# The last part's tail loads its weight chunks unsplit and splits them on the chip

## The chip, the cores and the metric

One core of a Trainium2 chip runs the whole kernel. The metric is the device time of one execution in microseconds (us); lower is better. Engine names follow the profile: PE is TensorE, DVE is VectorE, ACT is ScalarE, POOL is GpSimd, SP is SyncE, which here only issues transfers (DMAs).

## The reference

One step of a decoder layer for 1024 prompt tokens and 32 sample tokens with 1024 features, all in float32:

```
h = rms_norm(x);  z = h @ w_in                     # attention (8 heads) and a gated recurrence (4 heads)
x += concat([rms_norm(A), gated B]) @ w_out        # w_out 1024 x 1024
x += cross_attention(rms_norm(x), mem) @ w_co      # w_cq 1024 x 512, w_co 512 x 1024
h3 = rms_norm(x);  q = h3 @ w_pq                   # w_pq 1024 x 2048: 8 heads x 2 x 128
s1, s2 = q[..., :128] . k1, q[..., 128:] . k2      # top 16 of each, then top 16 of their sums
x += sum over 8 heads x 16 experts of  softmax(score) * gelu(h3 . peer_u[e]) * peer_v[e]
y = rms_norm(x)
```

## The kernel before

Products in float32 are made of three faster products: `split` (L168) writes a rounded copy `hi` (ACT, L169) and the rest `lo = src - hi` (DVE, L170), and `mm3` adds hi.hi, hi.lo and lo.hi (L201 to L203). The 1024 prompt tokens are handled in three parts of three, two and three blocks of 128 (the 32 sample tokens belong to the second). Each part has a middle (attention and recurrence) and a tail: w_out, w_cq, cross-attention, w_co, the norm h3, and then 16 chunks of w_pq, each followed by a product with the keys and `top16` on DVE (L917 to L921). In each tail a weight chunk is `project`ed at a time.

`load_w` (L179) loads such a chunk in halves of 128 x 512. The first part loads the weights themselves, splits them and stores both pieces in device memory (`wd`); the later parts load both stored pieces, in one DMA per half (L186), into the tile `wz` (three buffers in the last part). PE reads `wz` and nothing else touches it.

Beside the last part's tail run the last two `gates`: they turn the chosen experts of a block into a table, with two DVE instructions per four tokens (L1024, L1027), a PE product (L1032) and a copy (L1034), and store it (`gtall`). Five blocks of 128 tokens use all experts in the `dense` loop that follows: 128 steps, each with two halves: PE makes `a` (L201 to L203), ACT the gelu (L1088), DVE multiplies by the gate (L1090) and splits (L169, L170), PE adds into `y` and `yr` (L1098 to L1100). At its end the sums are normed and stored (L1138 to L1153). The other blocks (the sample tokens, then blocks 7, 6 and 5) fetch their experts a row of 128 x 1024 at a time: POOL issues an indirect DMA (L1183), DVE uses the row (L1190 for `peer_u`, L1201 for `peer_v`). These gathers run beside the end of the last tail and beside the dense loop; each block's own needs its experts chosen first (`select_tile`, which ends with L986). The sample's result is finished last (`finish_sample`, L1208).

The program is laid out ahead of time by a scheduler, which sets the order of each engine's queue from its own estimate; on the chip each engine works through its queue in that order. One `DVE` queue therefore serves the gates, the top 16, the gathers, the dense loop and the final norms.

## Time and profile before

| | us |
|---|---|
| median of 3 runs (lowest, highest) | 3629.08 (3626.5, 3631.28) |
| profiled execution, own time | 3627.68 |
| its span in the profile | 3625.8 |
| last part's tail: first and last stored-weight load of it issued | 1137.0 to 1726.0 |
| first and last gate multiply (L1090) of the dense loop | 1757.5 to 3562.5 |

The span is what the instructions cover; the own time is 1.9 us more. Times in the rows are counted from the span's start.

### The profile page before, as it was taken

How to read it: one execution, taken by the hardware profiler on the slowest of the kernel's cores; microseconds unless marked ns; L12 is line 12 of the kernel's file. 1: busy time of each engine (PE TensorE's matmuls, PEld its weight loads, DVE VectorE, ACT ScalarE, POOL GpSimd, SP SyncE). 2: the span in 40 equal slices, each digit the busy share in tenths (PEclk: the TensorE clock that was granted, in tenths of full speed). 3: DMA queues.
4: the chain of work that ended last, by engine and by line, in shares of the span. 5: the costliest groups of instructions: out<-in, count | busy, mean ns of one | idle time of the engine just before them, and what ended most of it. 6: DMA issues, size and time to landing. Idle time of an engine off the chain costs nothing.

```text
span 3625.8 us, 52725 instructions
## 1 busy us (share of the span) xinstructions
PE 3373.7 (93%) x19343; PEld 2912.4 (80%) x19343; DVE 2634.7 (73%) x5868; ACT 1220.6 (34%) x2282; POOL 1112.5 (31%) x871
## 2 busy tenths in 40 slices
PE   5999999999999889887799999999999999999994
PEld 4886776677887788777788998999888898988893
DVE  4443333243885687897888878988888898888997
ACT  4544344344434443431242222222222222222221
POOL 0000000000000000021316644656566565565555
PEclk9999999999999999898999999999999999999997
DMA  7667777656655485499659988999999999999998
GB/s 243 230 226 248 239 247 240 202 181 220 210 192 201 179 293 209 150 338 344 229 169 348 341 291 286 364 351 337 340 335 351 345 333 342 337 343 332 329 328 296
DMA packets 408514, 1007.82 MB, mean 278 GB/s; under 512 B 43968, under 2 KB 168896, under 8 KB 406848
## 3 DMA queue, kind: packets, MB, share of 16 engines
q1 hardware_dynamic: 288448, 568.20, 45.6%
q0 software_dynamic: 119808, 436.26, 33.0%
q8 instruction: 152, 2.49, 0.3%
q14 instruction: 106, 0.87, 0.1%
HBM read 866.01 MB, written 138.31 MB: 277 GB/s over the span
## 4 chain that ended last, share of the span: by engine, by line
PE 71%; DVE 10%; DMA 9%; issue 4%; ACT 3%; POOL 1%; SPq 1%; POOLq 0%; DVEq 0%; ACTq 0%
PE a L201 7%; PE a L203 7%; PE a L202 7%; PE y L1098 4%; PE y L1099 4%; PE y L1100 4%; PE z L201 4%; PE z L202 3%; PE z L203 3%; PE yr L1098 3%; PE yr L1099 2%; PE yr L1100 2%; PE y L201 2%; PE y L202 2%; PE y L203 2%
## 5 line engine op out<-in xcount | busy, mean ns | idle before, releaser
L1183 POOL DMA_INDIRECT row<-in_peer_u,ix x416 | 534.6, 1285 | 635.9 <-DVE dots L1190 347.6
L1183 POOL DMA_INDIRECT row<-in_peer_v,ix x416 | 543.1, 1306 | 412.1 <-DVE ha L1201 266.5
L201 PE MATMUL a<-xh,u 128*128 128x320 f32 x2048 | 636.8, 311 | 21.2 <-ACT w L1088 18.0
L203 PE MATMUL a<-xh,u 128*128 128x320 f32 x2048 | 634.5, 310 | 0.7 <-DVE u L170 0.7
L202 PE MATMUL a<-xl,u 128*128 128x320 f32 x2048 | 634.1, 310 | 0.0
L1201 DVE SCALAR_TENSOR_TENSOR ha<-row,dots,ha 128x1024 f32<-128x1024 f32 x416 | 533.0, 1281 | 22.2 <-DMA row<-in_peer_v,ix 17.8
L1190 DVE CUSTOM_DVE_ANT_0 row<-row,ha 128x1024 f32<-128x1024 f32 x416 | 497.9, 1221 | 39.5 <-DMA row<-in_peer_u,ix 39.5
L210 POOL TENSOR_TENSOR rs_r<-rs_m,mhalf 128x3 f32<-128x3 f32 (+2 forms) x25 | 23.4, 944 | 1369.7 <-DVE rs_m L208 1250.2
L1088 ACT ACTIVATE w<-a 128x320 f32<-128x320 f32 x256 | 111.6, 436 | 937.3 <-PE a L203 917.1
L201 PEld LDWEIGHTS a<-xh,u 128*128 128x128 f32 x2048 | 385.6, 188 | 40.5 <-ACT w L1088 25.8
L202 PEld LDWEIGHTS a<-xl,u 128*128 128x128 f32 x2048 | 385.7, 188 | 8.8
L203 PEld LDWEIGHTS a<-xh,u 128*128 128x128 f32 x2048 | 385.5, 188 | 2.8 <-DVE u L170 1.0
L201 PE MATMUL z<-zhi,wz 128*128 128x384 f32 (+2 forms) x928 | 330.4, 356 | 43.0 <-DMA wz<-wd_w_pq 16.2
L202 PE MATMUL z<-zlo,wz 128*128 128x384 f32 (+2 forms) x928 | 316.8, 341 | 3.4 <-DVE zlo L170 1.9
L203 PE MATMUL z<-zhi,wz 128*128 128x384 f32 (+2 forms) x928 | 314.0, 338 | 0.0
L1099 PE MATMUL y<-v,w 128*128 128x512 f32 x768 | 294.6, 392 | 0.0
L1098 PE MATMUL y<-v,w 128*128 128x512 f32 x768 | 269.6, 393 | 12.6 <-ACT v L169 11.2
L1100 PE MATMUL y<-v,w 128*128 128x512 f32 x768 | 264.5, 391 | 1.3 <-DVE w L170 1.2
L201 PEld LDWEIGHTS z<-zhi,wz 128*128 128x128 f32 x928 | 181.0, 195 | 87.3 <-issue 21.7
L1098 PE MATMUL yr<-v,w 128*128 128x512 f32 x512 | 201.8, 394 | 13.5 <-DVE ys L1127 11.7
L169 ACT CAST w<-w 128x320 fp32r<-128x320 f32 x256 | 117.8, 460 | 259.0 <-DVE w L1090 258.5
L1100 PE MATMUL yr<-v,w 128*128 128x512 f32 x512 | 199.9, 390 | 0.7 <-DVE w L170 0.7
(470 smaller groups left out, 6685.2 us busy)
## 6 DMA issues: line engine op xcount, KB each, us to landing
u<-in_uT SPq DMA_DIRECT2D x128, 512.0 KB, 7.0
v<-in_peer_v SPq DMA_DIRECT2D x128, 512.0 KB, 7.6
wz<-wd_w_in SPq DMA_DIRECT2D x112, 512.0 KB, 4.3
gt<-gtall SPq DMA_DIRECT2D x124, 320.0 KB, 10.8
wd_w_in<-wz SPq DMA_DIRECT2D x56, 512.0 KB, 3.2
gtall<-sg SPq DMA_DIRECT2D x34, 512.0 KB, 4.1
wd_w_pq<-wt SPq DMA_DIRECT2D x32, 512.0 KB, 3.1
wt<-wd_w_pq SPq DMA_DIRECT2D x32, 512.0 KB, 4.5
```

The source lines that it names most:

```text
L169: S.copy(hi, src)
L201: PE.matmul(out, lhsT=whi, rhs=xhi[:, c, sl], start=c == 0, stop=False)
L202: PE.matmul(out, lhsT=whi, rhs=xlo[:, c, sl], start=False, stop=False)
L203: ins = PE.matmul(out, lhsT=wlo, rhs=xhi[:, c, sl], start=False, stop=c == kc - 1)
L210: G.tensor_tensor(r, m, mhalf[:, :n], op=ALU.pow)
L1088: S.activation(ga[:, lo:hi], pa, AF.Gelu)
L1098: PE.matmul(o, lhsT=wh[:, sl], rhs=vh[:, ds], start=start and q == 0, stop=False)
L1099: PE.matmul(o, lhsT=wh[:, sl], rhs=vl[:, ds], start=False, stop=False)
L1100: PE.matmul(o, lhsT=wl[:, sl], rhs=vh[:, ds], start=False, stop=stop and q == len(ws) - 1)
L1183: G.indirect_dma_start(out=row, out_offset=None, in_=tab, in_offset=bass.IndirectOffsetOnAxis(ap=col(ix, j), axis=0))
L1190: V.tensor_tensor_reduce(row, row, hn, 1.0, 0.0, op0=ALU.mult, op1=ALU.add, accum_out=col(dots, j))
L1201: V.scalar_tensor_tensor(acc, row, col(dots, j), acc, op0=ALU.mult, op1=ALU.add)
```

## The change

Only the last part's tail changes (`pi == 2`). Its weights come by a new function `load_raw`: the weights themselves, a whole chunk in one DMA, into a buffer that attention no longer needs (`vn` for odd chunks, `kT` for even ones, one buffer each), and then one `split` per half into `wz`.

```
+    def load_raw(name, c, kc, tag):
+        raw = T(wk, [128, 8, 128], F32, "vn", 1) if c % 2 else T(wk, [128, 1024], F32, "kT").rearrange("p (c n) -> p c n", n=128)
+        SP.dma_start(raw[:, :kc], A[name][c])
+        out = []
+        for i in range(kc // 4):
+            w = T(wk, [128, 2, 4, 128], F32R, tag, 3)
+            split(w[:, 0], w[:, 1], raw[:, 4 * i : 4 * i + 4])
             out.append((w[:, 0], w[:, 1]))
         return out
...
             put = lambda name, kc, x, evac: [
-                project(load_w(name, c, kc, g["w"]), x, kc, N, lambda p: evac(c, p), g["bank"] + "y")
+                project((load_raw if pi == 2 else load_w)(name, c, kc, g["w"]), x, kc, N, lambda p: evac(c, p), g["bank"] + "y")
                 for c in range(A[name].shape[0])]
...
-                project(load_w("w_pq", jc, 8, g["w"]), h3, 8, N, lambda p: ANY.tensor_copy(q[:, :N], p),
+                project((load_raw if pi == 2 else load_w)("w_pq", jc, 8, g["w"]), h3, 8, N, lambda p: ANY.tensor_copy(q[:, :N], p),
                         g["bank"] + "y")
```

With it the scheduler lays out the queues anew from the last tail on. In the changed kernel lines from L194 on have numbers 10 higher.

SP's queue in the middle of the last tail's w_pq chunks, before (`wd_w_pq` are the stored pieces, `xh`, `xl`, `u`, `gt` are the dense loop's first loads, `gtall` the gates' stores):

```order
L186 DMA wz_15166<-wd_w_pq_0_1462_6805 128x1024
L1036 DMA gtall_165<-thi_14723 128x2048
L186 DMA wz_15168<-wd_w_pq_1_1465_6812 128x1024
L186 DMA wz_15218<-wd_w_pq_0_1472_6867 128x1024
L1047 DMA xh_15700<-h3x_65_163 128x1280
L1047 DMA xl_15701<-h3x_66_164 128x1280
```

And the changed kernel at the same chunks:

```order
L199 DMA kT_15262<-in_w_pq 128x1024
L1046 DMA gtall_165<-sg_14353 128x1024
L1046 DMA gtall_165<-sg_14354 128x1024
L199 DMA vn_15318<-in_w_pq 128x1024
L199 DMA kT_15376<-in_w_pq 128x1024
L1046 DMA gtall_165<-thi_14455 128x2048
```

One load now brings a whole chunk where two did, and a load into `kT` or `vn` must wait until DVE has split what lay there.

DVE's queue just ahead of the dense loop's first gate multiply, before (`vals` and `f` are the top 16 of the last w_pq chunk, `tw`, `sc`, `ci` belong to the selection of block 5, `ha<-row` is a gather row of the sample):

```order
L921 MAX_INDEX vals_14850<-vals_14850,f_15670 128x8 x2
L949 CAST ixb_15961<-vals_14850 128x256
L917 MAX sc_15907<-tw_15909 128x8 x8
L1201 SCALAR_TENSOR_TENSOR ha_29739<-row_29768,dots_29642,ha_29739 128x1024
L918 MAX_INDEX ci_15908<-sc_15907,tw_15909 128x8 x2
L1090 TENSOR_TENSOR w_15744<-w_15744,gt_15725 128x320
```

And in the changed kernel (its gate multiply is L1100, its gather row L1211):

```order
L970 TENSOR_TENSOR tw_16107<-tw_16107,ixb_16097 128x2048
L972 TENSOR_TENSOR tw_16100<-tw_16100 128x128x4
L971 TENSOR_TENSOR tw_16107<-tw_16107 128x128x8
L959 CAST ixb_16270<-vals_14922 128x256
L973 TENSOR_REDUCE c_3339_16099<-tw_16100 128x128
L170 TENSOR_TENSOR v_15877<-v_15874,v_15876 128x1024
L1100 TENSOR_TENSOR w_15880<-w_15880,gt_15861 128x320
```

Nearly all of block 5's selection now stands ahead of the first gate multiply, where before it had only begun.

DVE's queue from the dense loop's last split of a gated half (`w`) on, before (`ha<-row` are gather rows, `ys` and `u` sums of the dense blocks, L1152 the scaling by a norm):

```order
L170 TENSOR_TENSOR w_29431<-w_29429,w_29430 128x320
L1201 SCALAR_TENSOR_TENSOR ha_31808<-row_32133,dots_31423,ha_31808 128x1024
L1127 TENSOR_TENSOR ys_3268_15716<-ys_3268_15716,yr_29517 128x512
L1148 TENSOR_SCALAR fst_29580<-fst_29580 128x1
L1201 SCALAR_TENSOR_TENSOR ha_31808<-row_32136,dots_31423,ha_31808 128x1024
L1201 SCALAR_TENSOR_TENSOR ha_31808<-row_32139,dots_31423,ha_31808 128x1024
L1201 SCALAR_TENSOR_TENSOR ha_31808<-row_32142,dots_31423,ha_31808 128x1024
L1127 TENSOR_TENSOR ys_3268_15716<-ys_3268_15716,yr_29534 128x512
```

And in the changed kernel:

```order
L170 TENSOR_TENSOR w_29567<-w_29565,w_29566 128x320
L1148 TENSOR_TENSOR u_29712<-u_29712,y_3299_15847 128x512
L1137 TENSOR_TENSOR ys_3304_15852<-ys_3304_15852,yr_29653 128x512
L1158 TENSOR_SCALAR fst_29716<-fst_29716 128x1
L1162 SCALAR_TENSOR_TENSOR u_29712<-u_29712,fst_29716,u_29721 128x1024
L1148 TENSOR_TENSOR u_29725<-u_29725,y_3300_15848 128x512
```

Before, gather rows of the last block stand between the final sums and norms; in the changed kernel none is left by then.

## Rows read from the trace of the kernel before

**Rows 1.** The page: busy time by engine, and its shares in 40 slices of the span.

```profile
PE 3373.7 (93%) x19343; PEld 2912.4 (80%) x19343; DVE 2634.7 (73%) x5868; ACT 1220.6 (34%) x2282; POOL 1112.5 (31%) x871
...
DVE  4443333243885687897888878988888898888997
...
DMA  7667777656655485499659988999999999999998
```

**Rows 2.** Busy time in stretches from the last tail to the dense loop.

```profile
core 0: us, PE busy (x) PEld busy (x) DVE busy (x) ACT busy (x) POOL busy (x), PEclk, DMA share, GB/s
...
1300.00:1417.00 117.00, 112.22 (x778) 106.13 (x778) 87.22 (x358) 37.07 (x103) 0.00 (x0) 0.94 0.76 261
1417.00:1569.00 152.00, 125.62 (x799) 116.70 (x797) 132.26 (x421) 66.69 (x148) 9.58 (x9) 0.90 0.52 185
1569.00:1668.00 99.00, 83.09 (x532) 78.37 (x532) 97.90 (x305) 33.91 (x72) 20.92 (x18) 0.93 0.96 359
1668.00:1758.00 90.00, 56.08 (x284) 51.06 (x283) 60.09 (x267) 12.65 (x23) 16.92 (x18) 0.82 0.85 297
...
1900.00:3560.00 1660.00, 1633.50 (x9126) 1477.58 (x9125) 1431.40 (x1956) 430.29 (x707) 973.98 (x753) 1.00 0.93 335
```

**Rows 3.** The stored weights by tile: the last tail's loads, and who waited.

```profile
L186 SPq DMA_DIRECT2D wz<-wd_w_out x16: 319/320/1130, 1137.0 to 1430.1; - x16
...
L186 SPq DMA_DIRECT2D wz<-wd_w_cq x8: 319/319/320, 1433.7 to 1468.6; - x8
...
L186 SPq DMA_DIRECT2D wz<-wd_w_co x8: 319/320/722, 1472.4 to 1554.8; - x8
...
L186 SPq DMA_DIRECT2D wz<-wd_w_pq x32: 319/320/3084, 1559.4 to 1726.0; - x32
...
  PE z L201: 16.2, 6
```

**Rows 4.** Groups by line up to 1137 us: the same split, in the first part (busy, mean ns).

```profile
L170 DVE TENSOR_TENSOR wz<-raw,wz 128x512 fp32r<-128x512 f32 x56 | 38.7, 691 | 73.3 <-ACT wz L169 69.1 <-DMA wd_w_in<-wz 2.8 <-DMA raw<-in_w_in 1.2
...
L169 ACT CAST wz<-raw 128x512 fp32r<-128x512 f32 x56 | 34.6, 618 | 52.0 <-PE z L203 27.7 <-DMA raw<-in_w_in 11.6 <-DVE hq L452 6.8
```

**Rows 5.** DVE in order of time, in the last tail: two 128x512 instructions in succession.

```profile
1631.01 0.69 DVE L1024 TENSOR_TENSOR raw<-iota,x_vs 128x512 f32<-128x512 f32 x1
1631.61 0.69 DVE L1027 TENSOR_TENSOR oh<-high,low 128x512 f32<-128x512 f32 x1
```

**Rows 6.** DVE in order of time: adding the fifth chunk of w_out, in the last tail.

```profile
1417.33 0.56 DVE L551 TENSOR_TENSOR res<-z,res 128x384 f32<-128x384 f32 x1 [1.30 <-PE z L203]
```

**Rows 7.** Groups by line from 1430 us: a gather row, and two kinds of selection work.

```profile
L1201 DVE SCALAR_TENSOR_TENSOR ha<-row,dots,ha 128x1024 f32<-128x1024 f32 x416 | 533.0, 1281 | 22.2 <-DMA row<-in_peer_v,ix 17.8
...
L960 DVE TENSOR_TENSOR tw<-tw,ixb 128x2048 bf16<-128x2048 bf16 x10 | 12.2, 1222 | 0.0
...
L919 DVE MATCH_REPLACE8 tw<-sc,tw 128x100 f32<-128x100 f32 x42 | 10.0, 246 | 0.0
```

**Rows 8.** The gate multiplies by line: count, durations, first and last start.

```profile
L1090 DVE TENSOR_TENSOR w<-w,gt x256: 468/491/549, 1757.5 to 3562.5; 128x320 f32<-128x320 f32 x128
```

**Rows 9.** DVE, SP's queue and PE in order of time, from the last split on.

```profile
3565.34 0.54 DVE L170 TENSOR_TENSOR w<-w,w 128x320 fp32r<-128x320 f32 x1
...
3574.60 1.28 DVE L1152 SCALAR_TENSOR_TENSOR u<-u,fst,u 128x1024 f32<-128x1024 f32 x1
...
3588.90 1.28 DVE L1152 SCALAR_TENSOR_TENSOR u<-u,fst,u 128x1024 f32<-128x1024 f32 x1
...
3602.17 1.28 DVE L1201 SCALAR_TENSOR_TENSOR ha<-row,dots,ha 128x1024 f32<-128x1024 f32 x1 [1.46 <-DMA row<-in_peer_v,ix]
...
3604.75 1.28 DVE L1152 SCALAR_TENSOR_TENSOR u<-u,fst,u 128x1024 f32<-128x1024 f32 x1
...
3606.98 0.72 SPq L1210 DMA_DIRECT2D u<-accd  x1
...
3613.74 1.89 PE L1214 MATMUL yr<-u,sum 128*32 128x512 f32 x2 [34.88 <-DMA u<-accd]
```

More of the change, by code (lines that the diff above doesn't have):

```diff
@@ L193, in load_w @@
                     SP.dma_start(wd[name, c, i], w.bitcast(F32))
+            out.append((w[:, 0], w[:, 1]))
+        return out
+    def load_raw(name, c, kc, tag):
[5 more added lines that the diff above has]
+            split(w[:, 0], w[:, 1], raw[:, 4 * i : 4 * i + 4])
             out.append((w[:, 0], w[:, 1]))
```

## The prediction

> **What bounds the kernel now.** I read the page first. Over the whole span PE is busy 93% and DVE 73%, but both are averages: from about the middle on DVE and the transfers stand at eight or nine tenths in nearly every slice [rows 1]. So I cut the span into stretches around the changed tail [rows 2]. Up to 1417 us PE sets the pace (112 of 117 us), and DVE has 30 us idle. From 1417 to 1569 DVE is busy 132.3 of 152 us, idle 19.7. From 1569 to 1668 it is busy 97.9 of 99: DVE is full there, with the gates, the top 16 and the gathers in one queue, while the transfers too are at 0.96. From 1668 until the first gate multiply at 1757.5, DVE idles 29.9 of 90 us; here PE waits 16.2 us in six waits for stored w_pq pieces [rows 3], and the other engines wait behind it. So the last tail is bound by DVE's queue up to 1668 and by the weight loads after it. From the first gate multiply on PE rules: it is busy 1633.5 of 1660 us [rows 2], and the 256 gate multiplies come 1805/255 = 7.08 us apart [rows 8]. Whatever delays the first of them delays them all. At the end it is DVE's queue again, in which 21 gather rows stand behind the last split (counted in the order), and final norms between them [rows 9].
>
> **What is removed.** The last tail issues 16 + 8 + 8 + 32 = 64 loads of 512 KB, 33.6 MB [rows 3]. They become 36 (8, 4, 8 and 16; those of w_co hold 256 KB), 16.8 MB. At the 359 GB/s of 1569 to 1668 that is 47 us of transfer time less, but only its w_pq half falls where transfers are short.
>
> **What is added.** 64 splits of 128 x 512. On ACT a cast takes 0.62 us, 40 us in all [rows 4]; ACT is busy 33.9 of 99 us in the full stretch [rows 2], so that is hidden, unless a cast waits for its load at the head of ACT's queue. On DVE the subtraction takes 0.69 us [rows 4], and two such instructions in succession start 0.60 apart [rows 5]: 64 x 0.60 = 38.4 us.
>
> **What moves.** I counted DVE's new order up to the first gate multiply. Beside the splits it holds six more gather rows, at 1.2 each (1.28 less the overlap of 0.08) 7.2 us [rows 7]; most of block 5's selection, 30 top-16 instructions at about 0.25 and index work of which four take 1.14 [rows 7], in all about 16; and six evacuation copies that ACT made before, about 3. With the splits: 65 us more DVE work ahead of the first gate multiply. The six rows and the selection are work that DVE no longer has to do later, but later PE sets the pace, so doing it early gives nothing back there.
>
> **Delay of the dense loop.** About 4 of the 65 us stand ahead of the fifth w_out chunk at 1417.33 [rows 6], where PE is the slower one and DVE has room: nothing. The other 61 fall into 1417 to 1758, with 50.7 us of DVE idle to take them. Which idle can be used? The 29.9 us after 1668 come from late weights; with half the bytes, and w_pq chunks split several chunks ahead of their top 16 in the new order, I let 25 of them go. The 19.7 us before 1569 are waits for ACT's exponentials in cross-attention and for the first gather row; some splits now stand in between, so I take half, 10. Against that stand new waits of a subtraction for its cast: 56 such splits in the first part waited 69.1 us for ACT, 1.2 each, where DVE had nothing else to do [rows 4]. The bounds are 0 and 79 us; in a queue that is full the cast is usually done by the time DVE gets there, so I take the low end, 4. Delay: 61 - 25 - 10 + 4 = 30 us. Its bounds: all idle used, 61 - 50.7 = 10; only 25 used and 15 of cast waits, about 50.
>
> **The end.** From the end of the dense loop's last split (3565.9) to the span's end at 3625.8 there are 59.9 us. Each of the three norms of the kept blocks ends behind gather rows (scalings at 3574.60, 3588.90 and 3604.75), and the sample's finish can only load its sum after the third (3606.98) and runs to the end [rows 9]. In the new order no gather row is left there: 21 x 1.2 = 25.2 us of DVE work is gone from the chain. The norms still follow each other through ACT, POOL and a store each, so I take 36 us for what remains (bounds 34.7, if all 25.2 come off, and 45): 24 us less. This is the return of the gathers having gone ahead by those rows relative to the dense loop.
>
> **The dense loop itself** then holds about 20 gather rows more. DVE has 229 us idle in 1660 there and the transfers are at 0.93 [rows 2], 20 rows are 24 us of DVE and 10.5 MB. Hidden would be 0; all on the path 24. I take 4.
>
> **Sum.** +30 - 24 + 4 = +10 us. The profiled execution's own time is 3627.7, so 3637.7; the median of the runs stands 1.4 above it, so the median after is about 3639, 0.3% slower.
>
> **Rivals.**
> *The loads were the bound (faster).* PE waits for weights are the only waits in this tail that the change aims at. If the 61 us of DVE work could all slip into idle time (with casts and gathers never late), the delay would be 10 us or less, the sum -10 to -20: 3609 to 3619. The point that decides is a delay of 13 us: below it the time falls by over 0.2%. For it speak the 16.2 us of PE waits and DMA at 0.96; against it the stretch with DVE at 97.9 of 99, which has 1.1 us to give.
> The Trainium skill, Perfetto Trace Analysis, "Identifying the Most-Contended Engine", says to look for the engine with the highest occupancy and improve that one. Read over the whole span that is PE and the added DVE work costs nothing, which would make this rival the forecast, at about 3609; its "Optimization Strategy" adds that the most contended engine can change between regimes, and the rows by stretch show DVE at 99% in one of them, so I side with the stretch.
> *It cancels.* A delay of 13 to 27 us against the 24 at the end: within 0.2% (7 us), which is about what a measurement of this kernel can tell from no change. About 3629.
> *The raw buffers hold the queues (much slower).* `kT` and `vn` have one buffer each. A load waits for DVE's split of two chunks before; SP stands still meanwhile, and the gates' stores and the dense loop's first loads are queued behind it; ACT's cast at the head of its queue holds back the copies that empty PE's banks. With 15 us of waits for casts and no idle recovered before 1569, the delay is 50: 3660. For it speaks that DVE is the late engine, so each buffer comes free late; against it, that the loads stand four to six chunks ahead of the top 16 they serve.
>
> **Chances.** The forecast (delay 27 to 40, 3636 to 3650) 0.46; cancelled 0.26; faster 0.14; much slower 0.14. Slower by over 0.2%: 0.60; within: 0.26; faster: 0.14. Range for 8 in 10: from the middle of the faster rival to the slower one's own time, 3614 to 3660.
>
> **What would show it.** DVE near full from about 1417 until the first gate multiply, that multiply at about 1787 (1770 to 1800) instead of 1757.5, and PE's wait for w_pq weights gone or turned into a wait for the split. The gate multiplies 7.1 us apart as before, the last one about 30 later. The last gather row ahead of the last split, and some 36 us from there to the end. I would be wrong if DVE still had 30 us idle near the end of the tail, if the first multiply came before 1770, if the multiplies drew apart (the gathers then press on the loop), or if the end still took 50 us or more.

## The result and the profile after

The change makes the kernel slower: 3662.22 us (median of 7 runs, 3648.0 to 3672.07) against 3631.28 (7 runs, 3626.5 to 3639.34), a ratio of 1.0081 with a 95% interval of 1.0061 to 1.01. The profiled execution took 3665.35 us, with a span of 3663.6, which is 37.8 more than before; by the medians it is 30.9 more. Lines behind line 193 stand ten lower than in the kernel before (L1090 is L1100 now, L1024 is L1034).

The page, as [rows 1]:

```profile
PE 3401.0 (93%) x19343; PEld 2930.7 (80%) x19343; DVE 2675.8 (73%) x5939; ACT 1256.2 (34%) x2339; POOL 1114.3 (30%) x871
```

Busy time in stretches, as [rows 2], with one more for what is now ahead of the first gate multiply:

```profile
1417.00:1569.00 152.00, 126.71 (x795) 117.25 (x794) 143.15 (x460) 78.66 (x169) 11.64 (x8) 0.91 0.38 132
1569.00:1668.00 99.00, 81.60 (x504) 76.73 (x503) 93.32 (x221) 38.33 (x76) 24.54 (x21) 0.91 0.80 286
1668.00:1758.00 90.00, 63.59 (x331) 60.00 (x330) 85.66 (x346) 25.07 (x51) 20.24 (x20) 0.82 0.68 241
1758.00:1789.00 31.00, 7.26 (x26) 6.59 (x27) 30.03 (x133) 9.35 (x9) 3.55 (x3) 0.54 0.96 300
1900.00:3560.00 1660.00, 1614.80 (x8942) 1452.62 (x8942) 1412.87 (x1932) 424.86 (x694) 977.97 (x748) 0.99 0.92 332
```

DVE's idle time of 1668 to 1758 is gone (4.3 us in place of 29.9), the transfers fell from 0.96 to 0.80 in the full stretch, and none of PE's waits for w_pq pieces is left (16.2 us before). The splits are there, near the 691 ns that [rows 4] gave (half of the added tiles, durations in ns as least/median/most; 12 of the 64 stand ahead of the fifth w_out chunk), and so are the fifth w_out chunk, as [rows 6], and the gate multiplies, as [rows 8]:

```profile
L170 DVE TENSOR_TENSOR wz<-kT,wz x32: 666/678/693, 1154.3 to 1729.9; 128x512 fp32r<-128x512 f32 x32
```

```profile
1419.69 0.56 DVE L561 TENSOR_TENSOR res<-z,res 128x384 f32<-128x384 f32 x1 [0.76 <-PE z L213]
```

```profile
L1100 DVE TENSOR_TENSOR w<-w,gt x256: 472/489/510, 1788.7 to 3624.2; 128x320 f32<-128x320 f32 x128
```

The first gate multiply comes 31.2 us later than before, the last 61.7 later. So the loop between them, 1805.0 us before, takes 1835.6. The end, as [rows 9]:

```profile
3625.99 0.49 DVE L170 TENSOR_TENSOR w<-w,w 128x320 fp32r<-128x320 f32 x1
...
3645.22 0.78 SPq L1220 DMA_DIRECT2D u<-accd  x1
...
3651.66 1.89 PE L1224 MATMUL yr<-u,sum 128*32 128x512 f32 x2 [10.13 <-DVE ys L1162]
```

From the end of the last split to the span's end there are 37.1 us (59.9 before). From the last gate multiply to the span's end it is 39.4 in place of 63.3, 23.9 less. The three parts add up: +31.2 + 30.5 - 23.9 = +37.8.

Two views take the two large parts apart. The first is the stretch from the fifth w_out chunk to the first gate multiply, and then the loop. Before:

```profile
1417.33:1757.50 340.17, 263.96 (x1607) 245.30 (x1606) 289.75 (x988) 113.25 (x242) 46.93 (x45) 0.89 0.74 265
1757.50:3562.54 1805.04, 1774.44 (x9905) 1604.86 (x9904) 1562.47 (x2303) 490.17 (x786) 1015.52 (x776) 1.00 0.90 323
```

After:

```profile
1419.69:1788.65 368.96, 276.11 (x1637) 257.53 (x1635) 350.08 (x1150) 150.10 (x299) 59.98 (x51) 0.86 0.62 215
1788.65:3624.24 1835.59, 1787.89 (x9912) 1610.40 (x9913) 1566.68 (x2249) 485.79 (x783) 1028.96 (x786) 0.99 0.90 322
```

In the tail DVE does 60.3 us more (350.1 against 289.8) and idles 18.9 us in place of 50.4; the stretch grows by 28.8. In the loop PE idles 47.7 us in place of 30.6 and is busy 13.4 longer, over almost the same matmuls.

Which wait ends last ahead of the loop can be read too. PE's longest wait in the tail (us in total, times, the longest), and ACT's queue ahead of what PE waits for, after:

```profile
PE a L211 <- ACT u L169: 22.0, 1, 22.0
```

```profile
1776.15 0.40 ACT L977 ACTIVATE c<-c,rs 128x128 f32<-128x128 f32 x1 [16.92 <-DVE c L976]
1776.45 1.88 ACT L966 COPY tw<-abb 128x2048 bf16<-128x2048 bf16 x1
1778.24 1.04 ACT L169 CAST u<-u 128x1024 fp32r<-128x1024 f32 x1
```

ACT stands 16.9 us with an instruction of block 5's selection, for which DVE has not yet made the input. The loop's first cast of u is behind it, and PE waits 22.0 us for that cast. So in the changed kernel the last wait ahead of the loop is one for DVE's queue, not for a load. Before, it was one for DVE as well, that of the first GELU:

```profile
1754.60 0.44 ACT L1088 ACTIVATE w<-a 128x320 f32<-128x320 f32 x1 [17.71 <-DVE ixb L949]
```

The second view is what ACT waited for between 1800 and 3550 (us in total, times, the longest). Before:

```profile
ACT v L169 <- DMA v<-in_peer_v: 38.4, 19, 5.7
ACT u L169 <- DMA u<-in_uT: 36.8, 15, 6.3
```

After:

```profile
ACT v L169 <- DMA v<-in_peer_v: 66.8, 22, 10.7
ACT u L169 <- DMA u<-in_uT: 42.5, 13, 13.7
```

So the loop's loads of u and v come later, and two of the waits are over 10 us long (6.3 at most before). The longest in order of time, on ACT and on SP's queue:

```profile
2262.92 1.04 ACT L169 CAST u<-u 128x1024 fp32r<-128x1024 f32 x1 [13.74 <-DMA u<-in_uT]
```

```profile
2237.23 10.19 SPq L1074 DMA_DIRECT2D gt<-gtall  x4
2247.52 2.74 SPq L174 DMA_DIRECT2D u<-in_uT  x1
```

A u load leaves SP only behind four gate pieces. SP waited 3.2 us for the buffer of the first of them and took 10.2 us to issue the four; the u load itself took 2.7 us to issue (0.33 is the median of such issues), and its cast could start 12.7 us after that. ACT stands 13.7 us with the cast of u at the head of its queue; the GELU behind it, which empties PE's bank, waits too, and PE stops for 6.6 us. Most of this wait lies behind the issue, in the transfer.

### The profile page after: what moved, and what is told of

Its sections match the earlier page's. It is cut to its first block, busy times and chain, and to the rows that moved or that the text cites. A ratio compares the mean times of both kernels' runs of the same rounds, so it can differ in the third digit from the quotient of the medians.

```text
span 3663.6 us, 52824 instructions
## 1 busy us (share of the span) xinstructions
PE 3401.0 (93%) x19343; PEld 2930.7 (80%) x19343; DVE 2675.8 (73%) x5939; ACT 1256.2 (34%) x2339; POOL 1114.3 (30%) x871
## 4 chain that ended last, share of the span: by engine, by line
PE 71%; DVE 11%; DMA 8%; issue 5%; ACT 3%; POOL 1%; SPq 0%; POOLq 0%; DVEq 0%; ACTq 0%
PE a L211 7%; PE a L213 7%; PE a L212 6%; PE y L1108 4%; PE y L1109 4%; PE y L1110 4%; PE z L211 3%; PE z L212 3%; PE z L213 3%; DMA u<-in_uT 3%; PE y L211 2%; PE yr L1108 2%; PE yr L1109 2%; PE yr L1110 2%; PE y L212 2%
## 5 line engine op out<-in xcount | busy, mean ns | idle before, releaser
L1193 POOL DMA_INDIRECT row<-in_peer_u,ix x416 | 554.7, 1333 | 580.6 <-DVE dots L1200 314.5
L1193 POOL DMA_INDIRECT row<-in_peer_v,ix x416 | 528.4, 1270 | 471.4 <-DVE ha L1211 309.2
L1211 DVE SCALAR_TENSOR_TENSOR ha<-row,dots,ha 128x1024 f32<-128x1024 f32 x416 | 532.5, 1280 | 7.4 <-DMA row<-in_peer_v,ix 3.6
L220 POOL TENSOR_TENSOR rs_r<-rs_m,mhalf 128x3 f32<-128x3 f32 (+2 forms) x25 | 23.9, 964 | 1376.1 <-DVE rs_m L218 1067.3
L211 PE MATMUL z<-zhi,wz 128*128 128x384 f32 (+2 forms) x928 | 328.1, 354 | 30.5 <-ACT zhi L169 10.2
L1108 PE MATMUL y<-v,w 128*128 128x512 f32 x768 | 301.1, 392 | 9.6 <-ACT w L169 9.5
L1109 PE MATMUL y<-v,w 128*128 128x512 f32 x768 | 300.5, 391 | 0.0
L1110 PE MATMUL y<-v,w 128*128 128x512 f32 x768 | 245.6, 391 | 0.7 <-DVE w L170 0.6
```

The costliest lines, as they stand in the source:

```text
L211: PE.matmul(out, lhsT=whi, rhs=xhi[:, c, sl], start=c == 0, stop=False)
L220: G.tensor_tensor(r, m, mhalf[:, :n], op=ALU.pow)
L1108: PE.matmul(o, lhsT=wh[:, sl], rhs=vh[:, ds], start=start and q == 0, stop=False)
L1109: PE.matmul(o, lhsT=wh[:, sl], rhs=vl[:, ds], start=False, stop=False)
L1110: PE.matmul(o, lhsT=wl[:, sl], rhs=vh[:, ds], start=False, stop=stop and q == len(ws) - 1)
L1193: G.indirect_dma_start(out=row, out_offset=None, in_=tab, in_offset=bass.IndirectOffsetOnAxis(ap=col(ix, j), axis=0))
```

## The experiments

Theories. For the delay: (B) VectorE's added work, as forecast; against it (A), that the dense loop's x loads, first issued at 1743.09 in place of 1651, start the loop late. For the loop's stretch, which was not forecast: that gather rows running some 20 further ahead press on it; that its late start with no loads ahead does; that raw loads or splits do; that the order of SP's queue does. "Tail" below is the stretch from the fifth w_out chunk to the first gate multiply (340.2 before, 369.0 after), "loop" from the first to the last gate multiply, "end" from there to the span's end. All are of one profiled execution, which can lie some 10 us from its program's median (after_gtpool's took 3633.6 of 3640.4 us, after_e112's 3685.3 of 3673.9), and two profiles of one program differ by up to 5 us in the tail and 10 in the loop. Ratios are to the kernel before on the same chip; medians in different rows can be of different chips.

| kernel | tail | loop | end | median, us | ratio, 95% interval |
|---|---|---|---|---|---|
| before | 340.2 | 1805.0 | 63.3 | 3631.3 | |
| before_again | 344.8 | 1801.9 | 64.1 | 3635.2 (one run) | |
| before_e60 | 342.0 | 1801.5 | 52.2 | 3616.0 | 0.9949 (0.9934 to 0.9965) |
| before_u6 | 343.6 | 1811.7 | 64.6 | 3637.0 | 0.9997 (0.9981 to 1.0013) |
| before_u6_e60 | 337.2 | 1787.9 | 57.6 | 3606.1 | 0.9907 (0.9891 to 0.9924) |
| before_gtpool | 330.9 | 1788.9 | 73.0 | 3613.8 | 0.9939 (0.9915 to 0.9963) |
| before_gtpool_e60 | 329.3 | 1782.7 | 65.2 | 3598.9 | 0.9889 (0.9867 to 0.9911) |
| before_hold | 349.2 | 1817.2 | 49.6 | 3638.5 | 1.0002 (0.9988 to 1.0016) |
| stored_split | 360.8 | 1797.6 | 59.4 | 3639.1 | 1.0005 (0.9987 to 1.0023) |
| raw_rest | 355.7 | 1814.1 | 55.1 | 3645.1 | 1.0015 (0.9999 to 1.0032) |
| after | 369.0 | 1835.6 | 39.4 | 3662.2 | 1.0081 (1.0061 to 1.01) |
| after_again | 368.6 | 1826.1 | 40.4 | 3661.9 (one run) | |
| after_e112 | 365.5 | 1840.5 | 50.3 | 3673.9 | 1.0093 (1.0064 to 1.0122) |
| after_u6 | 365.7 | 1799.6 | 55.3 | 3642.3 | 1.0019 (1.0004 to 1.0034) |
| after_ufirst | 362.3 | 1823.6 | 52.0 | 3655.5 | 1.0066 (1.0043 to 1.009) |
| after_gtpool | 366.3 | 1790.0 | 61.2 | 3640.4 | 1.0028 (1.0014 to 1.0041) |
| raw_top | 381.6 | 1806.1 | 43.0 | 3659.7 | 1.0059 (1.0039 to 1.0079) |
| no_sub | 357.2 | 1827.0 | 40.8 | 3652.1 | 1.0046 (1.0024 to 1.0069) |
| sub_pool | 377.9 | 1826.5 | 40.9 | 3672.3 | 1.0103 (1.0064 to 1.0142) |
| no_rest | 347.7 | 1810.4 | 43.7 | 3634.8 | 0.9993 (0.998 to 1.0007) |

**no_sub and sub_pool: the subtraction left out, or on GpSimd.**

Both in the changed kernel, first no_sub, then sub_pool:

```diff
-            split(w[:, 0], w[:, 1], raw[:, 4 * i : 4 * i + 4])
+            S.copy(w[:, 0], raw[:, 4 * i : 4 * i + 4])
+            S.copy(w[:, 1], raw[:, 4 * i : 4 * i + 4])
```

```diff
-            split(w[:, 0], w[:, 1], raw[:, 4 * i : 4 * i + 4])
+            S.copy(w[:, 0], raw[:, 4 * i : 4 * i + 4])
+            G.tensor_tensor(w[:, 1], raw[:, 4 * i : 4 * i + 4], w[:, 0], op=ALU.subtract)
```

> The changed kernel with the 64 subtractions of its last tail left out: the rest part of each weight is a second cast by ScalarE of the raw chunk (the product is then not the reference's; this part of the computation is changed). VectorE loses 64 x 0.60 = 38 us ahead of the first gate multiply, the loads and the single raw buffers stay. If VectorE's added work is the delay, the first gate multiply (1788.7 in the changed kernel, 1757.5 in the one before) comes at 1750 to 1762. If late raw loads, or raw buffers that come free late, are the delay, it stays at 1780 or more. The dense loop (first to last gate multiply, 1805 us before, 1835.5 in the changed kernel) keeps its 1835 if its stretch belongs to the gather rows that run some 20 rows further ahead of it, since in this order they still do (829 rows ahead of the last gate multiply, 832 in the changed kernel, 810 before); it goes back to 1805 if the late start or the subtractions stretched it. By the first theory of both the whole is 3630 us; with late loads and the stretch gone 3630 too, so that only the two stretches tell them apart.

> The changed kernel with the 64 subtractions of its last tail on GpSimd in place of VectorE. No run so far shows GpSimd's price for a 128x512 subtraction; GpSimd is busy 20 to 40 of 100 us there, in gather issues alone. If VectorE's queue is the delay and GpSimd's price is 2 us or less, the first gate multiply comes at 1750 to 1770 and the whole at 3630 to 3640, and 25 us under that if the dense loop does not stretch. If GpSimd's subtractions hold up its gather issues, or each takes over 4 us, the first gate multiply is at 1800 or later and the whole over 3670.

no_sub did neither: first gate multiply at 1778.3, tail 357.2, so 11.8 us of the 28.8 came back, and the loop kept most of its stretch. It is not a clean test, since 64 more casts stand in ACT's queue and DVE took over copies that ACT made. sub_pool is slower than the change itself. GpSimd takes 1.4 us a piece, within what was allowed, but some of VectorE's own instructions grow while it works. Groups by line in 1417 to 1780 (count, busy us, mean ns), the gates' first comparison in the changed kernel, and then the same here with a group of GpSimd's, which is of 1100 to 1790:

```profile
L1034 DVE TENSOR_TENSOR raw<-iota,x_vs 128x512 f32<-128x512 f32 x77 | 52.1, 678 | 0.1
```

```profile
L1035 DVE TENSOR_TENSOR raw<-iota,x_vs 128x512 f32<-128x512 f32 x78 | 65.9, 846 | 4.0 <-PE g L1043 3.1 <-PE x L1043 0.4 <-PE y L1043 0.2
L204 POOL TENSOR_TENSOR wz<-vn,wz 128x512 fp32r<-128x512 f32 x32 | 47.0, 1467 | 209.9 <-ACT wz L203 196.2 <-DMA gtall<-sg 13.6
```

So VectorE is busy 351.9 us in this tail (350.1 in the changed kernel's), although the 52 subtractions that fell into it, 31 us, are gone.

**before_e60 and after_e112: the gathers' lead.**

before_e60 is the kernel before with this edit, after_e112 the changed kernel with 112 in place of 60:

```diff
-EARLY = 90
+EARLY = 60
```

> The kernel before with one number changed: the gather rows get their five further buffers from row 60 on, not from row 90 on. The order up to the first gate multiply is the same (41 rows ahead of it); from the 60th gate multiply on the gathers run 9 to 18 rows further ahead (205 against 187 at the 65th, 514 against 502 at the 161st, 819 against 810 at the last; 206, 526 and 832 in the changed kernel). If the lead of the gathers over the dense loop is what stretches it, the loop takes 1820 to 1830 us here (1805 before), the end after it shrinks by 10 us, and the whole is 3635 to 3645. If the stretch belongs to the raw loads or the later start, the loop stays at 1805, and with a shorter end the whole is 3615 to 3625.

> The changed kernel with one number changed: the further gather buffers come from row 112 on, not from row 90 on. The first gate multiply keeps its place (1788.7); the gathers' lead over the dense loop falls by 5 to 16 rows (200 against 206 at the 65th gate multiply, 515 against 526 at the 161st, 719 against 736 at the 225th, 820 against 832 at the last). If the lead stretches the loop, it takes 1815 to 1825 us (1835.5 in the changed kernel), the end grows from 39 to 50, and the whole is 3652 to 3662. If the lead has nothing to do with it, the loop stays at 1835 and the whole is 3670 to 3680.

Both went the other way. With a greater lead the loop of the kernel before took 1801.5 us, and with a smaller one that of the changed kernel took 1840.5. So a lead of this size is not what stretches the loop, and my theory of it fell.

**before_hold, raw_rest, raw_top: entry loads or work.**

before_hold, in the kernel before, behind w_pq's product:

```diff
+                if pi == 2 and jc == 15:
+                    V.tensor_copy(T(wk, [128, 1024], F32, "kT")[:, :8], q[:, :8])
+                    V.tensor_copy(T(wk, [128, 8, 128], F32, "vn", 1)[:, 0, :8], q[:, :8])
```

raw_rest, in the changed kernel:

```diff
-                project((load_raw if pi == 2 else load_w)("w_pq", jc, 8, g["w"]), ...
+                project(load_w("w_pq", jc, 8, g["w"]), ...
```

raw_top, in the changed kernel:

```diff
-        raw = T(wk, [128, 8, 128], F32, "vn", 1) if c % 2 else T(wk, [128, 1024], F32, "kT")...
+        raw = T(wk, [128, 8, 128], F32, "rw", 2)
...
-            p = wl if tag in LONG else wr if tag == "res" else we
+            p = wl if tag in LONG else wr if tag in ("res", "rw") else we
```

> The kernel before, stored parts and all, with two copies of 128x8 added: after the last w_pq chunk one number column block is copied into each of the buffers kT and vn, so that these two stay in use to the end of the last tail, as they do in the changed kernel. Theory A, entry loads: the dense loop's x lies where those buffers were, so its loads (first issued at 1651 in the kernel before, at 1743 in the changed one) wait for the end of the tail; the first gate multiply came 45 us after the first x load in the changed kernel and in no_sub, sub_pool and after_e112 alike. Then the first x load is issued at 1728 to 1740 here and the first gate multiply comes at 1772 to 1785. Theory B, VectorE's work: no work worth naming is added, the first gate multiply stays at 1757.5. On the dense loop: if it is stretched by its late and empty-handed start, it takes 1820 to 1835 us here too and the whole is 3650 to 3665; if by something that the raw loads alone bring, it stays at 1805, and the whole is 3632 to 3645 under A and 3630 under B.

> The change for three of the four matrices only: w_out, w_cq and w_co of the last tail are loaded themselves and split (32 splits, 19 us of VectorE), w_pq comes as stored parts as before. kT and vn are free before w_pq begins, and in this order the x loads stand among the w_pq loads again. Theory A: the first x load comes at 1655 to 1670, the first gate multiply at 1757 to 1768, the dense loop takes 1800 to 1815, and the whole is 3620 to 3640. Theory B: half the splits bring about half the delay, the first gate multiply comes at 1768 to 1778 and the whole is 3640 to 3650.

> The changed kernel with its raw chunks in two buffers of their own, outside the memory that the dense loop's x takes. The order of SyncE's queue is unchanged in this: the x loads still stand behind all w_pq loads. Theory A, first form (the buffers' memory holds the x loads): SyncE's wait of 14 us ahead of the first x load goes, it is issued at 1726 to 1732, the first gate multiply comes 45 us later at 1771 to 1777 and the whole is 3640 to 3652. Theory A, second form (SyncE's order alone holds them, or the gates that end at 1698 do): first x load 1726 to 1745, first gate multiply 1771 to 1790. Theory B: the first gate multiply stays at 1788.

before_hold does what A said: the x loads come late, and the first gate multiply 43.9 us behind them (SP's queue in order of time, and the tail by its busy time):

```profile
1728.70 0.32 SPq L1050 DMA_DIRECT2D xh<-h3x  x1
```

```profile
1423.38:1772.61 349.23, 258.12 (x1598) 241.22 (x1596) 311.75 (x1081) 119.39 (x247) 49.24 (x47) 0.87 0.75 262
```

But the price is 9 us of tail, little over the scatter (337 to 345 us in five profiles of the four programs that share the kernel before's tail), and it came with 22 us more VectorE work in it, since in the new order the wait was filled with selection work. The other two speak against A as a rule: in raw_rest, where 32 of the 64 splits are left, x is issued at 1672.5 and the first gate multiply comes 103 us later (its tail is 15.5 us longer than before, about half of the 28.8, with 312.6 us of VectorE work), in raw_top at 1729.7 and 70 us later, 13 us earlier than in the changed kernel and the multiply 11.5 later. raw_top has the most work on VectorE of the three, 357.7 us. Its loop, though, takes 1806.1 us with the changed kernel's raw loads and splits, in another order, and with a still later start. So neither of these stretches the loop by itself.

**stored_split and no_rest: the work without the loads, the loads without the work.**

stored_split, in the kernel before (`keep` is 2 in the last tail; `zero` is a column of zeros, made once at the start):

```diff
                 SP.dma_start(w.bitcast(F32), wd[name, c, i])
+                if keep == 2:
+                    S.copy(w[:, 0], w[:, 0])
+                    V.tensor_tensor(w[:, 1], w[:, 1], zero, op=ALU.add)
```

no_rest, in the changed kernel:

```diff
-            split(w[:, 0], w[:, 1], raw[:, 4 * i : 4 * i + 4])
-            out.append((w[:, 0], w[:, 1]))
+            S.copy(w[:, 0], raw[:, 4 * i : 4 * i + 4])
+            out.append((w[:, 0], w[:, 0]))
```

> The kernel before, loading the stored parts as before, with the changed kernel's work added and nothing else: behind each of the last tail's 64 loads a cast of the rounded part onto itself on ScalarE and a sum of the rest part with zero on VectorE. The x loads stand among the w_pq loads as in the kernel before. Theory B (VectorE's work delays the dense loop): 64 x 0.60 = 38 us more on VectorE, of which some 25 to 30 us of its 50 us of idle time between 1417 and 1757 can take a part: first gate multiply at 1768 to 1785, whole 3640 to 3655. Theory A (only the late entry loads delay it): first gate multiply at 1757 to 1763, whole 3630 to 3638.

> The changed kernel with the 64 subtractions of its last tail left out and nothing put in their place: the rounded part stands in for the rest part in the third product (so this part of the computation is changed). Raw loads, buffers and casts are those of the changed kernel, and the x loads stand behind all w_pq loads. Theory A: the x loads are issued at 1720 to 1735 and the first gate multiply comes 44 to 46 us later, at 1765 to 1780, with VectorE's work gone. Theory B: the first gate multiply comes at 1750 to 1760. If both hold the loop back about equally, 1765 to 1780 too, but then stored_split must be at 1768 or later. The dense loop: 1800 to 1840, by the place of its u loads in the new order.

The two agree. Adding the work lengthens the tail by 20.6 us (360.8 against 340.2); taking it from the change shortens it by 21.3 (369.0 to 347.7). The rows of stored_split and then of no_rest:

```profile
1417.39:1778.19 360.80, 279.69 (x1601) 257.71 (x1602) 324.32 (x1045) 140.70 (x294) 50.59 (x47) 0.86 0.72 253
```

```profile
1420.91:1768.61 347.70, 262.24 (x1598) 244.78 (x1596) 320.31 (x1084) 145.21 (x288) 53.30 (x52) 0.89 0.66 228
```

So some 21 of the 28.8 us belong to the subtractions (16 of them by before_again's tail of 344.8). The other 7.5 stay without them: VectorE still has 30.6 us more to do than before (gathers, selection and copies that the order moved ahead), and the x loads are late. Neither run leaves all else alone: stored_split also has 64 casts more on ACT, and its x loads come at 1686.3, 35 us later than before. Its loop took 1797.6 us: splits do not stretch it.

**after_u6 and before_u6: a sixth buffer for u,** here and where else the tag is used.

```diff
-            uhl = load_split(dn, [128, 8, 128], A["uT"][i], "u", 5)
+            uhl = load_split(dn, [128, 8, 128], A["uT"][i], "u", 6)
```

> The changed kernel with six buffers for u in the dense loop in place of five. ScalarE waited 110 us for u and v loads in the changed kernel's loop (75 in the kernel before), up to 13.7 us at a time, and SyncE 224 us for VectorE's splits of u (178 before) ahead of such loads. If late u loads are what stretches the loop, it takes 1800 to 1815 us (1835.5 with five) and the whole is 3635 to 3650. If the loads are late because the transfers are full, a sixth buffer changes little: 1825 to 1840, 3655 to 3670. The first gate multiply stays at 1788 either way.

> The kernel before with six buffers for u in the dense loop in place of five. In the changed kernel the sixth took the loop from 1835.5 to 1799.6 us. If it takes away what the change's order brought and no more, the loop of the kernel before has little to gain: 1798 to 1806 (1805 with five), whole 3620 to 3636. If u loads are late in every order, it gains here too: loop 1775 to 1790, whole 3600 to 3615. First gate multiply at 1757 in both.

In the changed kernel the loop went back to 1799.6 us; in the kernel before it did not gain (1811.7, ratio 0.9997). ACT's waits for u and v were still 98 us in after_u6's loop (109 in the changed kernel's), and one of them 13.4. In before_u6 they were 130 us with a loop of 1811.7, in raw_top 93 us, with waits of 10.6 and 9.8 among them, and a loop of 1806.1. So ACT's waits for u and v do not set the loop's length by themselves, and a sixth buffer is no cure in every order.

**after_again and before_again: the same programs once more.** No edit.

> The changed kernel itself, profiled once more. If the stretch of the dense loop belongs to its order, the loop takes 1825 to 1840 us again, and ScalarE's waits of over 5 us for u and v stand at the same steps (13.7 us at 2262, 10.7 at 3133, 6 to 6.5 at 2026, 2380, 2844 and 3248). If it is chance, the long waits stand elsewhere and the loop may be as short as 1810.

> The kernel before itself, profiled once more: first gate multiply at 1757 within 5 us, loop 1800 to 1812, end 61 to 65. ScalarE's longest waits for u and v were 5.5 to 6.3 us. If the loop's length is chance, it can be anywhere between 1800 and 1830.

The long waits stand at the same steps again (ACT in order of time, after_again):

```profile
2266.16 1.04 ACT L169 CAST u<-u 128x1024 fp32r<-128x1024 f32 x1 [12.86 <-DMA u<-in_uT]
...
3129.91 1.05 ACT L169 CAST v<-v 128x1024 fp32r<-128x1024 f32 x1 [10.42 <-DMA v<-in_peer_v]
```

The loop took 1826.1 us, and 1801.9 in before_again. The stretch belongs to the program; its size is 24.2 and 30.5 us by these two pairs. Of the seven waits of over 5 us for u and v in after_again, six can be followed to a load and its landing: each of these loads was issued behind four gate pieces, with at most one other load between them, and landed 12.8 to 18.8 us after its issue began. The u and v loads of 1800 to 3550 (issue to landing in us, least/median/most), and the gate pieces (issue in ns), in after_again:

```profile
DMA to landing us min/median/max: 3.3/7.2/19.6
...
L1074 SPq DMA_DIRECT2D gt<-gtall x120: 377/534/6776, 1840.0 to 3506.6; - x120
```

In before_again such loads land as late (up to 20.0 us), but no wait for them is longer than 6.7.

**after_ufirst, after_gtpool, before_gtpool: what stands ahead of u.**

after_ufirst, and then the edit of after_gtpool and before_gtpool:

```diff
-            gate_piece(k, 1 - h, i % 4)
             uhl = load_split(dn, [128, 8, 128], A["uT"][i], "u", 5)
+            gate_piece(k, 1 - h, i % 4)
```

```diff
-            ins = SP.dma_start(gts[k, h][:, ...
+            ins = (SP if k == 0 else G).dma_start(gts[k, h][:, ...
```

> The changed kernel with each step's u load issued ahead of its gate piece, not behind it (two lines of the dense loop change places). If u loads are late because they stand behind gate pieces that wait for their buffer (SyncE waited 181 us in 25 waits ahead of gate pieces in the loop), the loop takes 1800 to 1815 us and the whole is 3635 to 3650. If the stretch is not in that queue, 1825 to 1840 and 3655 to 3670. First gate multiply at 1785 to 1792 in both.

> The changed kernel with the dense loop's gate pieces, all but the first steps', issued by GpSimd in place of SyncE, so that SyncE's queue holds u and v alone. If gate pieces ahead of u loads are the cause, the loop takes 1795 to 1810 us. But GpSimd issues the gathers too, and these then stand behind the gate pieces: their lead shrinks (810 rows ahead of the last gate multiply, 832 in the changed kernel), and the end grows from 39 to 55 to 62 us. Whole 3645 to 3660. If SyncE's queue is not the cause, loop 1825 to 1840 and whole 3675 to 3690.

> The kernel before with the dense loop's gate pieces issued by GpSimd, as in after_gtpool. If SyncE's queue is what the two orders differ by, both loops come out alike: 1786 to 1794 us (1805 and 1835.5 with the pieces on SyncE, 1790 in after_gtpool). The gathers, behind the pieces, end later (797 rows ahead of the last gate multiply, 810 before): an end of 70 to 76 us in place of 63. First gate multiply at 1755 to 1768, whole 3615 to 3635. The changed kernel with this would then stand behind it by its delay less its shorter end, some 10 to 15 us. If the loop stays at 1800 to 1806, the queue is a price of the change alone.

To change the code's order left the loop at 1823.6 (1826.1 in after_again): in the queue that the scheduler wrote from it, late u and v loads still stand behind four gate pieces. To take the gate pieces out of SP's queue did shorten it: 1790.0 us in place of 1835.6 in the changed kernel, and 1788.9 in place of 1805.0 in the kernel before. The two loops are alike then. ACT's waits for u and v in after_gtpool, and the loop by its busy time:

```profile
ACT v L169 <- DMA v<-in_peer_v: 17.5, 6, 5.8
...
ACT u L169 <- DMA u<-in_uT: 5.8, 5, 3.4
```

```profile
1780.66:3570.62 1789.96, 1772.74 (x9912) 1611.21 (x9913) 1538.96 (x2225) 483.25 (x781) 1108.31 (x889) 1.00 0.91 324
```

before_gtpool:

```profile
1748.41:3537.32 1788.91, 1773.61 (x9911) 1610.69 (x9911) 1550.72 (x2294) 490.70 (x786) 1118.42 (x886) 1.00 0.91 323
```

The transfers still run at 323 to 324 GB/s, as before (322 to 323), so no bandwidth was won. But three things went at once with the pieces. SP no longer waits for their buffers (181 us of 1900 to 3500 in the changed kernel, 189 in the kernel before). It no longer issues them (143 us in the changed kernel's loop, up to 6.9 us for one). And they no longer travel in one DMA queue with u and v: GpSimd's transfers run in another, q0, and in larger packets. All packets of 1800 to 3550 and SP's queue, q1 (packets, MB, share of the 16 engines' time), and issue to landing of u and v, of after_again and then of after_gtpool:

```profile
DMA packets 225848, 570.54 MB, mean 326 GB/s; under 512 B 20809, under 2 KB 96457, under 8 KB 225729
q1 hardware_dynamic: 116879, 172.58, 28.8%
```

```profile
DMA packets 158150, 569.67 MB, mean 326 GB/s; under 512 B 18209, under 2 KB 19489, under 8 KB 158029
q1 hardware_dynamic: 38454, 135.43, 21.1%
...
DMA to landing us min/median/max: 3.4/6.8/11.3
```

Nearly 80000 small packets are gone from SP's queue, and no u or v load of which the trace has the landing came later than 11.3 us after its issue (19.6 in after_again). Which of the three shortened the loop was not tested. SP's wait for the buffers alone does not tell the two orders apart, as it was no shorter in the kernel before. The Trainium skill, DMA: Bandwidth & Descriptors, "Issuing engines are not separate DMA queues", says that issuing from several engines saves only the time to issue. The bandwidth here agrees; the loop's 16 and 46 us are no measure of that rule, because queue and packets changed with the engine.

With this, the change still costs 0.9% (ratios of 1.0028 and 0.9939 to the kernel before), as much as without it (0.8%): the stretch of the loop is gone, but the tail is 35.4 us longer than before_gtpool's and the end only 11.8 shorter.

**before_u6_e60 and before_gtpool_e60: better than both.** The numbers above together, in the kernel before.

> The kernel before with six buffers for u and the further gather buffers from row 60 on: the two numbers that experiments here found to help. before_e60 alone gave 3616 (0.9949 of the kernel before), by an end of 52 us in place of 63 and a loop of 1801.5. With both: first gate multiply 1757, loop 1797 to 1803, end 50 to 54, whole 3606 to 3618. If the sixth buffer only repairs late orders, it adds nothing to before_e60: 3612 to 3620.

> The kernel before with the gate pieces on GpSimd and the further gather buffers from row 60 on. Gathers 801 rows ahead of the last gate multiply (797 with 90): loop 1784 to 1794, end 63 to 72, whole 3608 to 3625. Against before_u6_e60 (3606) this tells whether a cleared queue is worth more than a sixth u buffer once the gathers have their buffers early.

Both beat the kernel before and the changed one. The fastest is before_gtpool_e60 at 3598.89 us (0.9889, 0.9867 to 0.9911), with a tail of 329.3, a loop of 1782.7 and an end of 65.2 us: the stored parts stay, the gate pieces go to GpSimd's queue, and the gathers get their five buffers 30 rows earlier.

## Why the prediction was right and wrong

**The sum** came out at +10 us; it was +37.8 in the profiled execution and +30.9 by the medians. The sign was right and the time, 3662 against 3639, was off by a single term.

**"Delay: 61 - 25 - 10 + 4 = 30 us": right.** It was 31.2 in all, 28.8 from the fifth w_out chunk on (26.3 and 23.8 between the second profiles). The term of 61 us of added VectorE work behind that chunk measured 60.3. The idle time that takes it, 35 less 4, measured 31.5 (50.4 to 18.9). One reading in it was wrong without effect: the 19.7 us of idle time before 1569 were 7.7 us of waits for gather rows, 7.0 for a product of PE and only 1.0 for ACT's exponentials; half of it was taken all the same (8.9 us are left). stored_split and no_rest put the 64 subtractions at 16 to 21 us of the delay, from two sides. With the wait that ends last, which is for VectorE's selection, they show that VectorE's work sets this stretch, where over the whole span VectorE is at 73%. What the forecast did not have, and its third rival did, is that the dense loop's first loads come later, x by 92 us. They are nearly as late as the work: in after_again the first u load landed at 1778.8, and its cast stood until 1783.2 behind the selection. before_hold, which brings that lateness with 22 us of VectorE work, costs 9 us (4 against before_again).

**"24 us less" at the end: right.** 36 us were forecast behind the last split, 37.1 were measured, and by the mechanism forecast: the last gather row is done by 3618.3, ahead of the last split at 3625.99.

**"The dense loop itself ... I take 4": the step that failed.** It measured +30.5 (24.2 between the two programs' second profiles), outside the bounds of 0 and 24 that I had given, or at their edge. I had priced the loop by the gather rows it holds more, as if nothing but their work and their bytes could change there. before_e60 and after_e112 show no such price of the rows' lead. The scheduler dealt the loop's queues anew, and the stretch stays with that program (after_again): in it, u and v loads that land late behind gate pieces are waited for up to 13.7 us, in the kernel before up to 6.7. With the gate pieces in another queue these waits fall to 23 us in all and the two loops are equal within 1.1 us. That the stretch belongs to this order, and not to the raw loads, the splits or the later start, is shown by raw_top, which has all three in another order and a loop of 1806.1. That the long waits are the whole of it is not shown, since after_u6 and raw_top have nearly as many and no such stretch. Of the 30.5 us, 17.1 are more idle time of PE. The 13.4 of longer busy time are open: summed over 1-us stretches, the lowered clock takes 6.7 us of busy time in the changed kernel's loop in place of 1.6, but it takes 6.7 in before_again's too, so this part comes and goes with the execution.

**The rivals.** That the raw buffers hold the queues gave 3660, the nearest number, but not by its own mechanism. The dense loop's first loads were held up as it says, but its 50 us of delay did not come; to take the buffers' memory out of the way (raw_top) shortened nothing in the tail.

**What stays open.** Why this order suffers more than the one before is not settled: SP waits ahead of gate pieces about as long in both (181 us in the changed kernel and 189 in the one before, between 1900 and 3500), and loads behind them land as late. Which part of moving the pieces helps, the freed queue of SP, the other DMA queue or the larger packets, is open as well. A run that only changed the pieces' packets, or issued them from another engine into the same DMA queue, could tell. Every edit deals all queues anew, so none of these runs changes one thing alone. Moving the pieces to GpSimd also holds the gathers back (810 rows, counted in the order, ahead of the last gate multiply in place of 832), so that part of the effect may be theirs, though after_e112, with 820, had none. The loop also differs among orders with the pieces on SP without a rule that I found, from 1788 to 1840 us.

## What to carry to other kernels

Price added work by the idle time of its engine in that stretch, not over the span: 31 us of subtractions in the stretch (38 in all) cost 16 to 21 here, and the delay forecast from the stretch, 30, measured 31 and 26. But where a scheduler writes the order of every queue, an edit deals the queues anew far behind it too, so give a long loop that follows a term of its own, with bounds as wide as that loop has been seen to vary among orders (some 50 us in 1800 here), not only what the edit's bytes and instructions bring. And look at who waits for loads in such a loop: in the changed kernel every long wait that could be followed was for a load issued right behind four loads of another kind in small packets. To give those another queue shortened the loop in both kernels, though it did not lower the price of the change.

## What was not expected of the hardware

**VectorE waits while GpSimd subtracts.** In sub_pool the gates' 128x512 comparison with two inputs took 846 ns on average in place of 678, but the mean hides two groups (ns as least/median/most):

```profile
L1035 DVE TENSOR_TENSOR raw<-iota,x_vs x78: 640/687/2406, 1417.2 to 1696.1; 128x512 f32<-128x512 f32 x78
```

66 of the 78 took at most 712 ns. The other 12 took 1293 to 2406, and each of these overlapped a subtraction on GpSimd. One of them, with its subtraction:

```profile
1481.46 1.29 POOL L204 TENSOR_TENSOR wz<-vn,wz 128x512 fp32r<-128x512 f32 x1 [3.77 <-ACT wz L203]
1482.00 1.29 DVE L1035 TENSOR_TENSOR raw<-iota,x_vs 128x512 f32<-128x512 f32 x1
```

It ends 0.54 us after the subtraction does, as if it had begun only then. FIND_INDEX8 kept its time (288 and 283 ns). The Trainium skill, SBUF — State Buffer, "SBUF: two separate sides", says that VectorE and GpSimd lock one pair of ports against each other, and that an instruction of VectorE with two inputs in SBUF takes part in this. The rows agree.

**The clock goes down in one wait.** In the changed kernel's wait for u, PE stops at 2257.7 and starts at 2264.35. Stretches of 1 us (columns as in [rows 2], granted clock third from the end):

```profile
2257.00:2258.00 1.00, 0.72 (x4) 0.26 (x2) 0.00 (x0) 0.00 (x0) 0.00 (x0) 1.00 1.01 398
2260.00:2261.00 1.00, 0.00 (x0) 0.00 (x0) 0.00 (x0) 0.00 (x0) 0.00 (x0) 0.89 0.80 319
2262.00:2263.00 1.00, 0.00 (x0) 0.00 (x0) 0.00 (x0) 0.08 (x1) 0.00 (x0) 0.50 0.04 16
...
2267.00:2268.00 1.00, 1.00 (x7) 1.00 (x6) 1.00 (x2) 0.31 (x1) 0.63 (x1) 0.70 0.81 324
2268.00:2269.00 1.00, 1.00 (x9) 1.00 (x9) 1.00 (x1) 0.00 (x0) 0.00 (x0) 1.00 0.71 143
```

The granted clock falls from 1.00 to 0.50, from the 2.4 to the 1.2 GHz level, while PE does nothing, and comes back to 1.00 at 2268, after it has worked again. So this late load cost more than its wait: PE worked some 3 us at the lower clock behind it.
